# A hybrid decoder trunk on one core: its last stage written as one list of tasks, with the last 512 rows leaving as rows

## The chip, the cores and the metric

One Trainium2 chip, of which the kernel uses one core. The metric is the device time of one execution in microseconds (us). TensorE (PE) multiplies, VectorE (DVE), ScalarE (ACT) and GpSimd (POOL) work on the results, and SyncE (SP) and ACT issue the transfers.

## The reference

Two layers over 1024 tokens of width 1024, all in float32: an RG-LRU block with a SwiGLU network, then stick-breaking attention with a SwiGLU network, and a last RMS norm.

```python
def rms_norm(x, g):
    y = xf * lax.rsqrt(jnp.mean(xf * xf, axis=-1, keepdims=True) + RMS_EPS)
    return y * g
def swiglu_ffn(x, w_in, w_out):
    gu = jnp.einsum("bsd,df->bsf", x, w_in)
    h = jax.nn.silu(gu[..., :D_FF]) * gu[..., D_FF:]
    return jnp.einsum("bsf,fd->bsd", h, w_out)
# per layer:
h = h + mixed                       # RG-LRU (layer 0) or attention (layer 1)
h = h + swiglu_ffn(rms_norm(h, ffn_norm[layer]), ffn_w_in[layer], ffn_w_out[layer])
# at the end:
return rms_norm(h, final_norm)
```

D_FF is 2816. What the change touches is the end of the last SwiGLU network (the product with ffn_w_out) and the last norm.

## The kernel before

The residual h lies in the on-chip memory transposed: tile `h[d][n]` holds 128 columns of the model (block d of 8) by 512 tokens (half n of 2). Every operand of a product is split into a high and a low part of reduced float32, and a product of two such operands is three matmuls (`mm3`: high by high, high by low, low by high), each 128x128 by 128x512 where nothing else is said.

The products of the two SwiGLU networks save one in eight by Strassen's scheme on 2x2 blocks (Winograd's form): seven products, numbered 0 to 6, for eight. A product is summed in a PSUM bank (`BANK`: products 0, 2, 4 and 5 follow one another in one bank, 3 and 6 in another, 1 in a third); behind each product `post_out` adds the bank to h, so the next product in a bank waits until that has been read. Weights are summed and split for them by `Weights` (s12, s2, s3, do_s4 make the sums; a_hi/a_lo, b_hi/b_lo, c_hi/c_lo, d_hi/d_lo the parts; tiles wah, wal, wbh, wbl, wch, wcl, wd). The second matrix is worked off in 13 visits (`VISITS`): visit (d, p0, p1) is the column blocks d and d + 4 with the planes p0 to p1 of the hidden width, a plane being two blocks of 128. A visit of four planes is 84 matmuls, of three 63. The planes' operands come by DMA from a scratch in HBM (`bring`, issued by SP as soon as PE has read the place for the last time) and are split by ACT and DVE (`split_op`: a cast `vh<-vl` and a subtraction) at fixed steps of a visit. The order of PE, ACT, DVE and POOL is that of the code, written out by hand; SP's is set by the scheduler of the language.

The last two visits of layer 1, (3, 8, 11) and (0, 9, 11), are worked off by `finish`: the first with the seven products, the second, with two planes, in plain products `last` (12 matmuls each), so that pieces of it fill PE while the norm is prepared. In it

- `finished(d, n)` squares h[d][n] on ACT, adds the square to `acc[n]` on DVE and multiplies h by the gain of the last norm on ACT;
- `stats` sums acc over the partitions with four one-column matmuls against ones (each counts as two in the trace) and works out the factor 1/rms of each token in a few small steps of DVE and one root of ACT (whose table is loaded at the start of `finish`);
- `factor` spreads the factors over the partitions by matmuls (tile `ob`), `give` multiplies h by them on DVE, or on POOL for some blocks, and stores h transposed (`out_t`).

The first 768 tokens leave the chip transposed. For the last 256, h is transposed on PE (`turn`, 16 transposes), the factor is multiplied in where the banks are read (`y`), and they leave as rows (`out_r`). The host puts the two parts together. `last` is done in three pieces of tokens: all of half 0, the first 256 of half 1, the last 256 of half 1, for the column blocks 0 and 4 each.

Of the kernel before, what the change touches and what calls it, by code (L numbers as in the profile page):

```python
# [16 lines left out]
P = 128  # L17
# [13 lines left out]
LATE = S - 2 * P  # L31
# [318 lines left out]

@with_exitstack
def trunk(
# [11 lines left out]
    ffn_w_out,  # L364
    out,
# [41 lines left out]
    vc = cp.tile([P, P], F32, name="vc")  # L407

# [121 lines left out]
    def gain(h, d, n):  # L530
        nc.scalar.activation(h[d][n], h[d][n], AF.Copy, scale=vc[:, V_FIN + d : V_FIN + d + 1])
# [37 lines left out]
    with ExitStack() as st, tc.manual_schedule(engines={E.PE, E.Activation, E.DVE, E.Pool, E.SP}):  # L569
# [79 lines left out]
        for j in range(3):  # L649
            V.tensor_scalar_mul(nbias[:, :, j], bin_rec, -1.0)  # L650
        column_stats(sacc[1], bank, 1)
# [233 lines left out]
    def mix_out_ffn_in(h, mix, bias, layer, gnext, ob):  # L885
# [131 lines left out]
        with tc.manual_schedule(engines={E.PE, E.Activation, E.DVE, E.Pool}):  # L1017
# [303 lines left out]
            def open_end():  # L1321
                gs.close()
                ep = gs.enter_context(tc.tile_pool(name="ends", bufs=1, reuse_waits="tile"))
                held.append(ep.tile([P, S], F32, name="held"))
                held.extend(ep.tile([P, D], F32R, name=f"we{i}") for i in range(4))
# [50 lines left out]
            def finish(w, e):  # L1376
                u, rs = NV - 2, held[0]
                d1, q0, q1 = VISITS[u]
                d0, p0, p1 = VISITS[u + 1]
                rhs = {i: [R[p][i] for p in range(q0, q1)] for i in range(NPROD)}  # L1380
                banks = {}

                def product(i):
                    new = BANK[i] not in banks
                    if new:
                        banks[BANK[i]] = pp.tile([P, NB], F32, tag="p", name=f"p{i}_ps")
                    part(banks[BANK[i]], w, i, rhs[i], range(len(rhs[i])), onto=not new)
                    return lambda: post_out(u, i, banks[BANK[i]])

                def last(x, n, i0, i1):  # L1390
                    cs = slice(i0 * P, i1 * P)
                    ps = pp.tile([P, NB], F32, tag="p", name="o_ps")[:, cs]
                    for k, p in enumerate(range(p0, p1)):
                        for y in range(2):
                            hi, lo = e.a[("r", y) if x else y]
                            c = slice(k * P, (k + 1) * P)
                            rhs_ = [t[:, cs] for t in R[p][((0, 1), (7, 6))[n][y]]]
                            mm3(ps, hi[:, c], lo[:, c], *rhs_, k + y == 0, k + y == 2)
                    t = h[d0 + x * HK][n][:, cs]
                    V.tensor_add(t, ps, t)  # L1400
                    nc.scalar.square(half(sq, n)[:, cs], t)

                def summed(x, n, i0, i1):
                    cs = slice(i0 * P, i1 * P)
                    t, ac = h[d0 + x * HK][n][:, cs], acc[n][:, cs]
                    V.tensor_add(ac, ac, half(sq, n)[:, cs])
                    nc.scalar.activation(t, t, AF.Copy, scale=vc[:, V_FIN + d0 + x * HK : V_FIN + d0 + x * HK + 1])

                def factor(n, i0, i1):
                    cs = slice(i0 * P, i1 * P)  # L1410
                    spread(half(ob, n), n, i0, i1)
                    nc.scalar.copy(half(rs, n)[:, cs], half(ob, n)[:, cs])

                def give(n, i0, i1, fast, slow=()):
                    cs = slice(i0 * P, i1 * P)
                    for d in (*slow, *fast):
                        t = h[d][n][:, cs]
                        if d in slow:
                            nc.gpsimd.tensor_mul(t, t, half(rs, n)[:, cs])
                        else:  # L1420
                            V.tensor_mul(t, t, half(ob, n)[:, cs])
                        lo = n * NB + i0 * P
                        nc.sync.dma_start(out_t[d][:, lo : lo + (i1 - i0) * P], t)

                first, mid, end = (0, 0, 4), (1, 0, 2), (1, 2, 4)
                root = cp.tile([P, 4], F32, tag="rs_s", name="rs_s", bufs=2)
                nc.scalar.sqrt(root[:, 0:1], ones)
                w.b_lo()
                post = product(0)
                post()  # L1430
                w.c_hi()
                w.c_lo()
                e.a_hi()
                post = product(1)
                post()
                e.a_lo()
                post = product(2)
                post()
                finished(d1, 0)
                w.d_hi()  # L1440
                w.d_lo()
                e.r_hi()
                e.r_lo()
                sq = rp.tile([P, D], F32, tag="raw", name="sq")
                last(0, *first)
                post = product(4)
                summed(0, *first)
                post()
                last(1, *first)
                post = product(5)  # L1450
                summed(1, *first)
                post()
                post = product(3)
                finished(d1 + HK, 0)
                post()
                last(0, *mid)
                stats(acc[0], pp, "p", 0)
                finished(d1 + HK, 1)
                summed(0, *mid)
                post = product(6)  # L1460
                factor(*first)
                give(*first, (), (3, 7))
                post()
                give(*first, (1, 2))
                last(1, *mid)
                finished(d1, 1)
                give(*first, (5,))
                summed(1, *mid)
                last(0, *end)
                give(*first, (0,), (4,))  # L1470
                summed(0, *end)
                stats(acc[1], pp, "p", 1, 0, 2)
                give(*first, (6,))
                last(1, *end)
                factor(*mid)
                give(*mid, (), (3, 7))
                summed(1, *end)
                rows = [(hf, i, pp.tile([P, NB], F32, tag="p", name="e_ps")) for i in range(2, 4) for hf in range(2)]

                def turn(js):  # L1480
                    for hf, i, ps in rows:
                        for j in js:
                            nc.tensor.transpose(
                                ps[:, j * P : (j + 1) * P], h[HK * hf + j][1][:, i * P : (i + 1) * P], ident
                            )

                turn((1, 2, 3))
                give(*mid, (1, 2))
                stats(acc[1], pp, "p", 1, 2, 4)
                turn((0,))  # L1490
                ys = [rp.tile([P, D], F32, tag="raw", name="y") for _ in range(2)]
                for k, (hf, i, ps) in enumerate(rows):
                    y = half(ys[i - 2], hf)
                    r = rcol[:, NT // 2 + i : NT // 2 + i + 1]
                    if k % 2 == 0:
                        nc.scalar.activation(y, ps, AF.Copy, scale=r)
                    else:
                        V.tensor_scalar_mul(y, ps, r)
                    (nc.scalar if k % 2 else nc.sync).dma_start(
                        out_r[(i - 2) * P : (i - 1) * P, hf * NB : (hf + 1) * NB], y  # L1500
                    )
                    if k == 1:
                        give(*mid, (5, 6), (0, 4))

            last_use = {p: max(u for u, (_, p0, p1) in enumerate(VISITS) if p0 <= p < p1) for p in range(NF // 2)}
            for s_, (kind, x) in enumerate(steps[:looped]):
                w, nw, ahead = nw, nxt, None
                if s_ + 2 < len(steps):
                    ahead = weights_of(*steps[s_ + 2])
                    if final and s_ + 3 == len(steps):  # L1510
                        ahead.homes = held[1:]
# [15 lines left out]
                for k, i in enumerate(ORDER):  # L1527
# [79 lines left out]
                    if kind == "v":  # L1607
# [22 lines left out]
            for dn in done:  # L1630
                finished(*dn)
            del done[:]
            if final:
                finish(nw, nxt)
# [364 lines left out]
```

## Time and profile before

| | |
|---|---|
| median of 3 runs | 2187.65 us (2184.54 to 2188.76) |
| the profiled execution, its own time | 2188.74 us |
| its span, first to last instruction | 2187.0 us |
| busy, of the span | PE 99%, weight loads 82%, DVE 78%, ACT 49%, POOL 2% |
| granted TensorE clock, mean | 0.996 |
| product 0 of `finish` starts, in the span | 2139.33 us |

Times of the trace are from the start of its span. In rows of the timeline the first two numbers are the start and the length of an instruction, and the bracket at the end tells how long the engine had been idle and what ended that. A matmul's length includes its way through the array, so successive matmuls overlap; their distance is what PE spends on one. PEld are PE's weight loads.

### The profile page before, as it was taken

The numbers are of one execution on the slowest core, as the hardware profiler recorded it, in microseconds if no ns is written. First come the engines' busy times: TensorE is split into PE (matmuls) and PEld (weight loads), VectorE is DVE, ScalarE is ACT, GpSimd is POOL, SyncE is SP. The second block draws the span as 40 slices with busy tenths as digits, with TensorE's granted clock in tenths as the row PEclk, the third lists the DMA queues.
The fourth block names the chain that finished last, engine by engine and source line by source line (L and its number), as shares of the span: only waits on it lengthen the run. The fifth ranks groups of instructions, "written<-read, shape, count | busy, mean of one in ns | idle before, by whom it ended". The sixth has DMA issues, their size and how long they took to land.

```text
span 2187.0 us, 27244 instructions
## 1 busy us (share of the span) xinstructions
PE 2165.4 (99%) x10054; PEld 1797.8 (82%) x10054; DVE 1707.1 (78%) x2434; ACT 1078.3 (49%) x1776; POOL 35.6 (2%) x44
## 2 busy tenths in 40 slices
PE   9999999999999999999999999999999999999997
PEld 7888888888888888877888888888888888888886
DVE  7978678677777887867888888878867777788786
ACT  5577445334444554644555555544533444454455
POOL 0000020000000000000000000002000000000001
PEclk9999999999999999999999999999999999999999
DMA  4111312344444853444333333541133444476442
GB/s 175 39 49 48 126 39 82 96 140 146 142 146 135 288 188 121 146 117 113 89 104 88 106 87 106 169 165 61 65 109 125 150 142 144 148 242 227 133 136 86
DMA packets 132598, 274.50 MB, mean 126 GB/s; under 512 B 15344, under 2 KB 22640, under 8 KB 132464
## 3 DMA queue, kind: packets, MB, share of 16 engines
q1 hardware_dynamic: 132032, 271.97, 38.4%
q8 instruction: 79, 1.29, 0.2%
q10 hardware_dynamic: 432, 0.79, 0.1%
q14 instruction: 55, 0.45, 0.1%
HBM read 176.75 MB, written 70.78 MB: 113 GB/s over the span
## 4 chain that ended last, share of the span: by engine, by line
PE 94%; DVE 3%; ACT 2%; DMA 0%; issue 0%; SPq 0%; DVEq 0%; ACTq 0%
PE p_ps L446 18%; PE p_ps L444 18%; PE p_ps L445 18%; PE qk_ps L444 4%; PE qk_ps L446 4%; PE qk_ps L445 4%; PE z_ps L1786 3%; PE av_ps L1834 3%; PE wt_ps L1817 3%; PE a_ps L445 3%; PE a_ps L446 3%; PE a_ps L444 3%; PE ob_ps L445 2%; PE ob_ps L444 2%; PE ob_ps L446 2%; PE g_ps L446 1%
## 5 line engine op out<-in xcount | busy, mean ns | idle before, releaser
L444 PE MATMUL p_ps<-vh,wbh 128*128 128x512 f32 x524 | 204.8, 391 | 2.0 <-ACT ta L1362 2.0
L446 PE MATMUL p_ps<-vh,wbl 128*128 128x512 f32 x524 | 204.9, 391 | 0.0
L446 PE MATMUL p_ps<-vh,wcl 128*128 128x512 f32 x524 | 204.1, 390 | 0.5 <-DVE wcl L977 0.5
L445 PE MATMUL p_ps<-vl,wbh 128*128 128x512 f32 x524 | 204.6, 391 | 0.0
L446 PE MATMUL p_ps<-vh,wal 128*128 128x512 f32 x524 | 204.1, 390 | 0.1
L444 PE MATMUL p_ps<-vh,wch 128*128 128x512 f32 x524 | 204.1, 389 | 0.0
L445 PE MATMUL p_ps<-vl,wch 128*128 128x512 f32 x524 | 203.9, 389 | 0.0
L445 PE MATMUL p_ps<-vl,wah 128*128 128x512 f32 x524 | 203.9, 389 | 0.0
L444 PE MATMUL p_ps<-vh,wah 128*128 128x512 f32 x524 | 203.8, 389 | 0.0
L1798 ACT ACTIVATE F<-z_ps 128x512 f32<-128x512 f32 (+3 forms) x188 | 91.6, 488 | 181.2 <-PE z_ps L1786 181.1
L963 ACT CAST wbh<-sb 128x1024 fp32r<-128x1024 f32 (+2 forms) x69 | 69.7, 1010 | 192.5 <-DVE sb L947 192.5
L1805 DVE TENSOR_TENSOR_SCAN F<-F,unit 128x128 f32<-128x128 f32 (+3 forms) x128 | 104.8, 819 | 56.8 <-ACT F L1798 56.3
L444 PE MATMUL qk_ps<-vh,whi 128*128 128x512 f32 x264 | 120.5, 456 | 0.6 <-ACT vh L524 0.6
L444 PEld LDWEIGHTS p_ps<-vh,wbh 128*128 128x128 f32 x524 | 98.6, 188 | 22.8 <-ACT ta L1362 2.5
L446 PEld LDWEIGHTS p_ps<-vh,wbl 128*128 128x128 f32 x524 | 98.8, 188 | 21.7 <-DVE wbl L967 1.2
L446 PEld LDWEIGHTS p_ps<-vh,wcl 128*128 128x128 f32 x524 | 98.3, 188 | 21.6 <-DVE wcl L977 1.3
L446 PEld LDWEIGHTS p_ps<-vh,wal 128*128 128x128 f32 x524 | 98.3, 188 | 21.2 <-DVE wal L958 1.0
L445 PEld LDWEIGHTS p_ps<-vl,wbh 128*128 128x128 f32 x524 | 98.7, 188 | 20.6
L445 PEld LDWEIGHTS p_ps<-vl,wah 128*128 128x128 f32 x524 | 98.4, 188 | 20.5
L445 PEld LDWEIGHTS p_ps<-vl,wch 128*128 128x128 f32 x524 | 98.4, 188 | 20.5
L444 PEld LDWEIGHTS p_ps<-vh,wah 128*128 128x128 f32 x524 | 98.4, 188 | 20.4
L444 PEld LDWEIGHTS p_ps<-vh,wch 128*128 128x128 f32 x524 | 98.4, 188 | 20.4
(375 smaller groups left out, 5481.0 us busy)
## 6 DMA issues: line engine op xcount, KB each, us to landing
raw<-in_ffn_w_in SPq DMA_DIRECT2D x88, 512.0 KB, 3.7
vl<-pd SPq DMA_DIRECT2D x128, 256.0 KB, 3.3
pd<-U SPq DMA_DIRECT2D x90, 256.0 KB, 2.3
raw<-in_ffn_w_out SPq DMA_DIRECT2D x28, 512.0 KB, 4.0
raw<-in_attn_w_qkv SPq DMA_DIRECT2D x24, 512.0 KB, 4.0
kh<-qh SPq DMA_DIRECT2D x64, 128.0 KB, 2.3
kl<-ql SPq DMA_DIRECT2D x64, 128.0 KB, 2.3
acc<-pd SPq DMA_DIRECT2D x28, 256.0 KB, 2.6
```

The costliest lines, as they stand in the source:

```text
L444: nc.tensor.matmul(ps, lhsT=wh, rhs=mh, start=first, stop=False, **kw)
L445: nc.tensor.matmul(ps, lhsT=wh, rhs=ml, start=False, stop=False, **kw)
L446: nc.tensor.matmul(ps, lhsT=wl, rhs=mh, start=False, stop=last, **kw)
L963: nc.scalar.copy(self.full(self.wb), self.full(self.sb))
L1786: nc.tensor.matmul(ps[:, 0:n], lhsT=lhsT, rhs=rhs, start=i == 0, stop=i == 1)
L1798: nc.scalar.activation(F, Z.pop(c)[:, 0:n], AF.Sigmoid, scale=-SC)
L1805: V.tensor_tensor_scan(rev, rev, unit[:, NB - n :][:, ::-1], 0.0, op0=ALU.mult, op1=ALU.add)
L1817: nc.tensor.transpose(tp[:, c : c + P], F[:, (kb % 4) * P : (kb % 4 + 1) * P], ident)
L1834: nc.tensor.matmul(ps[:, c:], lhsT=VV[q][:, kb, hx], rhs=t.pop(u)[:, c:], start=kb == 4 * G and i == 0, stop=kb == 3 and i == 1,)
```

## The change

The last two visits are written as a list of tasks with engine, assumed cost, dependences and rank (`end_plan`), from which the class `Plan` (used for the first stages before) makes the order of each engine. What is done differs as well:

- All of half 1, 512 tokens, now leaves as rows (`LATE` is 512). The second visit's product for half 1 (`lower`) takes the hidden planes as the stationary and the weights as the moving operand, 256 columns in two runs of 128, so that its result has tokens on the partitions, and sums it in the bank onto transposes of h made there just before (`turned`: 32 transposes instead of 16). Each of the four row blocks of 128 tokens then gets the sum of squares of those 256 columns from ACT (`row_sum`, a square with a sum output), root, factor, and its output in four pieces on DVE and ACT (`row_out`); the blocks are stored as 512 KB each, the last in two halves. The gains of columns 0 and 4 come in there, as a row `gr` loaded from a new input `fin`; for half 1 they carry a factor -0.5 that saves a step in the factor.
- Half 0 is done as before, but its eight multiplications are all on DVE, and stored one block (256 KB) at a time. POOL has no work in the stage.
- DVE adds each bank to h directly (`onto_h`); ACT no longer copies banks for it in this stage.
- The weights of the second visit have tiles of their own; their loads and the load of the table for the root are written in visit (2, 8, 11), the last before `finish`. In the order that comes out, the table load stands there, and the loads, and the cast of the high parts, stand in visit (3, 0, 4), seven visits earlier.
- A tile `tiny` of 256 bytes a partition is added among the constants.

```diff
-LATE = S - 2 * P
+LATE = NB
+def end_plan(plan, fn, d0, d1, left):
...
+    halved = plan.add("dve", 0.4, fn["half", 0], [], 8)
+    bl = plan.add("dve", 0.92, fn["b_lo", 0], [], 0)
+    for d, n in left:
+        normed(d, n, None, 3)
+    ch = plan.add("act", 0.95, fn["c_hi", 0], [bl], 6)
+    cl = plan.add("dve", 1.1, fn["c_lo", 0], [ch], 6)
+    el = []
+    for x in range(2):
+        eh = plan.add("act", 0.5, fn["e_hi", x], [], 1)
+        el.append(plan.add("dve", 0.62, fn["e_lo", x], [eh], 1))
+
+    p = prod(0, [], 0)
+    h = post(0, p, 2)
...
+    def finish_row(i, dep, tdep, r):
+        s = plan.add("act", 0.5, fn["rsum", i], [dep], r - 8)
+        m = plan.add("dve", 0.2, fn["rmean", i], [s, m1], r - 8)
+        t = plan.add("act", 0.22, fn["rroot", i], [s, m1], r - 8)
+        f = plan.add("dve", 0.6, fn["rfac", i], [t, m], r - 8)
...
+    for i in range(2, 4):
+        deps = [f6, m1] if i == 2 else muls
+        t = mm(0.86, ("T", i, (1, 2, 3, 0)), deps, 24 + 2 * i)
+        finish_row(i, mm(1.46, ("low", i), [], 24 + 2 * i), t, 24 + 2 * i)
...
+    tiny = cp.tile([P, 64], F32, name="tiny")
...
-                root = cp.tile([P, 4], F32, tag="rs_s", name="rs_s", bufs=2)
-                nc.scalar.sqrt(root[:, 0:1], ones)
...
+                def lower(i):
+                    ps = rows[i, 0][:, 0 : 2 * P].rearrange("p (x c) -> p x c", x=2)
+                    for k, y_ in order:
+                        ah, al = (t[:, i * P : (i + 1) * P] for t in R[p0 + k][(7, 6)[y_]])
+                        wh, wl = (flat(t)[:, :, 2 * y_ + k] for t in (hi, lo))
+                        kw = dict(start=False, skip_group_check=True)
+                        nc.tensor.matmul(ps, lhsT=ah, rhs=wh, stop=False, **kw)
+                        nc.tensor.matmul(ps, lhsT=ah, rhs=wl, stop=False, **kw)
+                        nc.tensor.matmul(ps, lhsT=al, rhs=wh, stop=(k, y_) == order[-1], **kw)
...
+                def row_sum(i):
+                    nc.scalar.activation(junk, rows[i, 0][:, 0 : 2 * P], AF.Square, accum_out=one(s4, i))
...
+                def row_store(i, js):
+                    c = slice(js[0] * P, js[-1] * P + P)
+                    dst = pairs(out_r[i * P : (i + 1) * P])[:, :, c]
+                    (nc.sync if js[0] == 0 else nc.scalar).dma_start(dst, pairs(y[i])[:, :, c])
...
+                end_plan(Plan(pe=0.0, act=0.3, dve=1.0, dma=0.0), Steps(acts), d0, d1, done).emit()
...
+                            d, p0, p1 = VISITS[NV - 1]
+                            for y in range(2):
+                                src = ffn_w_out[layer, d + y * HK][:, :, p0 * P : p1 * P]
+                                nc.sync.dma_start(held[5 + y].rearrange("p (y c) -> p y c", y=2), src)
+                            nc.sync.dma_start(held[3][:, 0 : 2 * P], fin.broadcast_to([P, 2 * P]))
+                            nc.scalar.sqrt(tiny[:, 62:63], ones)
```

PE's order in the stage is now: products 0, 1, 2, upper 0 (half 0 of column block 0), 4, upper 1 (of block 4), 5, 3, eight transposes, sums of half 0, two thirds of product 6, the spread, the rest of 6, two transposes, lower 0, two transposes, lower 1, sums of half 1, four transposes, then eight transposes and lower 2, and eight transposes and lower 3.

DVE at the start of the stage, before; `hh_0` is half 0 and `hh_1` half 1 of h, `acc` the sums of squares, `ta` the copy of product 0's bank, `we` are the parts of the second visit's weights.

```order
L1366 TENSOR_TENSOR hh_0_13011<-p_ps,hh_0_13011 128x512
L521 TENSOR_TENSOR acc_13016<-acc_13016,rbc_82 128x512
L521 TENSOR_TENSOR acc_13015<-acc_13015,rbc_81 128x512
L967 TENSOR_TENSOR wbl<-sb,wbh 128x2x384
L1366 TENSOR_TENSOR hh_0_13005<-ta,hh_0_13005 128x512
L977 TENSOR_TENSOR wcl<-s_18207,wch 128x384
```

DVE at the same place with the change:

```order
L1474 TENSOR_TENSOR hh_0_13014<-p_ps,hh_0_13014 128x512
L626 TENSOR_TENSOR acc_13019<-acc_13019,rbc_84 128x512
L1074 TENSOR_TENSOR wbl<-sb,wbh 128x2x384
L1607 TENSOR_TENSOR we_17124<-end_17127,we_17123 128x512
L1607 TENSOR_TENSOR we_17124<-end_17128,we_17123 128x512
L1504 TENSOR_TENSOR hh_0_13008<-hh_0_13008,p_ps 128x512
L1601 TENSOR_TENSOR acc_13018<-acc_13018,rbc_83 128x512
```

One addition to acc has moved behind the addition of product 0 to h, and both low parts of the second visit's weights have moved ahead of it; that addition reads the bank itself.

PE around the sums of half 1, before; `o_ps` is a bank of `last`, and of the two operands the one before the comma is the moving, the other the stationary one.

```order
L445 MATMUL o_ps<-vl_0_13076,we_17123 128x256
L446 MATMUL o_ps<-vh_0_13075,we_17122 128x256
L510 MATMUL st_ps<-ones,acc_13016 128x1 x2
L444 MATMUL o_ps<-vh_3_13543,we_17121 128x256
L445 MATMUL o_ps<-vl_3_13544,we_17121 128x256
```

PE around the sums of half 1 with the change; `e_ps` is a bank of a row block, and moving and stationary operand have changed places.

```order
L1533 MATMUL e_ps<-we_17124,vh_0_13078 128x256
L1534 MATMUL e_ps<-we_17123,vl_0_13079 128x256
L1540 MATMUL st_ps<-ones,acc_13019 128x1 x4
L1521 MATMUL e_ps<-ident,hh_1_13009 128x128
L1521 MATMUL e_ps<-ident,hh_1_13017 128x128
```

All four sums stand in one place, behind lower 0 and lower 1 and ahead of the last transposes of these two row blocks, where before two of them stood between two pieces of `last`, and the other two behind the transposes.

ACT in visit (3, 0, 4), before; the two copies into `held` are those of its products 3 and 4, the casts are of planes for the next visit.

```order
L1297 CAST vh_3_13535<-vl_3_13536 128x512
L1362 COPY held<-p_ps 128x512
L1297 CAST vh_0_13045<-vl_0_13046 128x512
L1297 CAST vh_1_13047<-vl_1_13048 128x512
L1362 COPY held<-p_ps 128x512
```

ACT at the same place with the change:

```order
L1404 CAST vh_3_13538<-vl_3_13539 128x512
L1470 COPY held<-p_ps 128x512
L1404 CAST vh_0_13048<-vl_0_13049 128x512
L1404 CAST vh_1_13050<-vl_1_13051 128x512
L1604 CAST we_17123<-end_17127 128x512
L1604 CAST we_17123<-end_17128 128x512
L1470 COPY held<-p_ps 128x512
```

The casts of the second visit's weights have come in ahead of the copy of product 4. Their loads stand in SP's queue among the loads of the planes, the second one behind the load of the plane whose place is freed within product 3.

More of the change, by code (lines that the diff above doesn't have):

```diff
@@ L1384, in product @@
                     new = BANK[i] not in banks
                     if new:
[L1386 to L1412, printed above, removed]
@@ L1439, in finish @@
[L1439 to L1469, printed above, removed]
@@ L1470, in finish @@
[L1470 to L1484, printed above, removed]
-                            )
@@ L1487, in finish @@
[L1487 to L1496, printed above, removed]
-                    else:
[L1498 to L1503, printed above, removed]
+                        banks[BANK[i]] = bank(f"p{i}_ps")
@@ new lines, in turned @@
+                def turned(i, js):
+                    for j in js:
+                        new = (i, j // 2) not in rows
+                        if new:
+                            rows[i, j // 2] = bank("e_ps") if i < 3 else half(ob, j // 2)
+                        for x in range(2):
+                            c = (2 * (j % 2) + x) * P
+                            nc.tensor.matmul(
+                                rows[i, j // 2][:, c : c + P], lhsT=h[j + HK * x][1][:, i * P : (i + 1) * P], rhs=ident,
+                                is_transpose=True, start=new and x == 0, stop=True, skip_group_check=True,
+                            )
@@ new lines, in sums, with mean @@
+                def sums(n):
+                    if n == 0:
+                        banks["st"] = bank("st_ps")
+                    for i in range(4):
+                        nc.tensor.matmul(
+                            banks["st"][:, 4 * n + i : 4 * n + i + 1],
+                            lhsT=acc[n][:, i * P : (i + 1) * P], rhs=ones, start=True, stop=True,
+                        )
+                def mean(n):
+                    V.tensor_scalar(
+                        m4[:, 4 * n : 4 * n + 4], banks["st"][:, 4 * n : 4 * n + 4], 1.0 / D, EPS, op0=ALU.mult, op1=ALU.add
+                    )
@@ L1629, in mix_out_ffn_in @@
                         open_last()
[L1630 to L1634, printed above, removed]
+            if not final:
+                for dn in done:
+                    finished(*dn)
+                del done[:]
+        if final:
+            with tc.manual_schedule(engines={E.PE, E.Activation, E.DVE, E.Pool, E.SP}):
+                finish(nw)
         gs.close()
```

204 lines of the change are left out of this document (173 added, 31 removed).

## The prediction

> **What bounds the kernel now.** I read the page first, then a table of busy time by stretch over the last stage, then the timelines of the engines at each gap of PE.
>
> ```profile
> span 2187.0 us, 27244 instructions
> PE 2165.4 (99%) x10054; PEld 1797.8 (82%) x10054; DVE 1707.1 (78%) x2434; ACT 1078.3 (49%) x1776; POOL 35.6 (2%) x44
> 2139.30:2143.50 4.20, 4.20 (x19) 3.19 (x17) 3.89 (x8) 3.17 (x5) 0.00 (x0) 1.00 0.13 29
> 2143.50:2145.60 2.10, 0.07 (x1) 0.00 (x0) 0.93 (x3) 2.08 (x5) 0.00 (x0) 1.00 0.19 67
> 2145.60:2149.30 3.70, 3.69 (x9) 2.91 (x10) 2.81 (x5) 1.29 (x3) 0.00 (x0) 0.54 0.01 4
> 2149.30:2169.30 20.00, 19.96 (x113) 17.32 (x112) 12.58 (x25) 11.28 (x21) 2.20 (x2) 1.00 0.00 2
> 2169.30:2172.40 3.10, 0.00 (x0) 0.00 (x0) 2.72 (x4) 1.46 (x3) 1.57 (x2) 1.00 0.84 313
> 2172.40:2176.50 4.10, 4.09 (x20) 3.81 (x21) 3.12 (x11) 1.55 (x4) 0.00 (x0) 0.59 0.61 222
> 2176.50:2178.90 2.40, 2.38 (x22) 2.14 (x20) 1.39 (x5) 0.98 (x3) 1.68 (x3) 0.99 0.27 99
> 2178.90:2183.40 4.50, 0.00 (x0) 0.00 (x0) 3.45 (x9) 1.37 (x2) 1.10 (x2) 1.00 0.81 282
> ```
>
> PE is busy for 99% of the span, so the change can only win where PE stands. After length, the columns are busy time of PE, PEld, DVE, ACT and POOL, then PE's granted clock, DMA share and GB/s. In the last 47.7 us, which the change rewrites, PE has two gaps, of 2.1 and 3.1 us, each with a stretch at about half clock behind it (0.54, 0.59), and a tail of 8.1 us (2178.9 to 2187.0) without it. What ended the gaps:
>
> ```profile
> 2145.61 0.63 PE L444 MATMUL p_ps<-vh,wbh 128*128 128x512 f32 x1 [2.03 <-ACT ta L1362]
> 2172.41 0.60 PE L510 MATMUL st_ps<-ones,acc 128*128 128x1 f32 x4 [3.14 <-DVE acc L1406]
> 2143.58 1.28 ACT L1427 ACT_TABLE_LOAD   x1
> 2144.99 0.57 ACT L1362 COPY ta<-p_ps 128x512 f32<-128x512 f32 x1
> 2169.68 1.74 DVE L521 TENSOR_TENSOR acc<-acc,rbc 128x512 f32<-128x512 f32 x1 [1.00 <-ACT rbc L520]
> 2167.10 3.77 POOL L1419 TENSOR_TENSOR hh<-hh,held 128x512 f32<-128x512 f32 x3 [638.20 <-ACT held L1412]
> ```
>
> The first gap: product 2 sums onto the bank of product 0, whose copy by ACT stands behind a table load. The second: the column sums of half 1 wait for DVE, where one addition took 1.74 us while POOL multiplied.
>
> **The first gap, after.** The table load moves into the visit before, and the bank is read by DVE alone. DVE's rows now decide:
>
> ```profile
> 2141.86 0.68 DVE L521 TENSOR_TENSOR acc<-acc,rbc 128x512 f32<-128x512 f32 x1
> 2143.46 0.95 DVE L967 TENSOR_TENSOR wbl<-sb,wbh 128x768 fp32r<-128x768 f32 x1
> 2145.58 0.69 DVE L1366 TENSOR_TENSOR hh<-ta,hh 128x512 f32<-128x512 f32 x1 [1.17 <-ACT ta L1362]
> 2146.19 0.55 DVE L977 TENSOR_TENSOR wcl<-s,wch 128x384 fp32r<-128x384 f32 x1
> 2139.33 0.39 PE L444 MATMUL p_ps<-vh,wah 128*128 128x512 f32 x1
> 2143.19 0.39 PE L446 MATMUL p_ps<-vh,wal 128*128 128x512 f32 x1
> ```
>
> A 128x512 addition is followed by the next after 0.61 us (2145.58 to 2146.19); wbl takes 0.87 by its width (0.95 less the 0.08 by which an addition's 0.69 overlaps its follower). DVE is free of the same addition at 2141.86 + 0.61 = 2142.47. Then come wbl (to 2143.34), two low parts of the last weights (2144.55) and the addition that frees the bank (0.69: 2145.24). PE starts product 2 at 2145.27 instead of 2145.61: only **0.34 us** gained. The two low parts, placed ahead by a plan that takes DVE as free 1.0 us after product 0's start when it is so 3.1 us after it (2139.33), replace the table load. The gap is then 1.7 us (from 2143.58). Does the clock fall behind it? It fell after 2.03 us; that row is the nearest, so I take that it falls, which costs what it costs now. If not, 3.41 us at half clock go, 1.7 us more gained. [...]
>
> **From product 2 to PE's last instruction.** Row durations:
>
> ```profile
> 2168.03 0.28 PE L444 MATMUL o_ps<-vh,we 128*128 128x256 f32 x1
> 2168.15 0.28 PE L445 MATMUL o_ps<-vl,we 128*128 128x256 f32 x1
> 2162.37 0.95 PE L510 MATMUL st_ps<-ones,acc 128*128 128x1 f32 x8
> 2165.34 1.05 PE L491 MATMUL ob<-ident,rcol 128*128 128x128 f32 x8
> 2176.57 1.47 PE L1483 MATMUL e_ps<-ident,hh 128*128 128x128 f32 x12
> ```
>
> A 512-column matmul comes every 0.227 us (18 of products 0 and 1 from 2139.33 to 2143.19), a 256-column one every 0.12, a transpose every 0.11 (1.47 less the last one's drain of some 0.16, by 12); four column sums take 0.85, four spreads 0.9. After: 60 matmuls of 512 columns (13.6: products 4, 5, 3 and 6 of 9, two upper blocks of 12), 48 of 256 (5.76), 32 transposes (3.5), two sums (1.7), one spread (0.9), in all 25.5 us. Before: the same 108 matmuls, 16 transposes, 6 spreads. What may still stop PE: the sums of half 0 wait for addition, square and addition behind product 5 (0.69 + 0.64 + 0.69, some 2.2 with hand-overs), under product 3 (2.04) and eight transposes (0.87), so 0.7 is spare. The factors of half 0 (some 1.5 behind the sums) lie under six matmuls (1.36): 0.2 of wait. The sums of half 1, today's 3.14 us, wait for the addition onto h of product 6, its square, two multiplications and the last addition, some 3.2 us behind product 6; under T, low 0, T, low 1 lie 3.3. Without that cover it costs up to the 3.1 of today. The eight multiplications of half 0 are all DVE's now, and POOL no longer slows it. So from product 2's end 25.7 us, where before it was 2149.27 to 2178.88, 29.6: **3.9 us** gained, mostly the 3.1 gap and the 1.7 behind it, less 16 transposes (1.8), with two spreads (0.45) and the short stalls between small matmuls on top.
>
> Last matmul: 2149.27 - 0.34 + 25.7, rounded 2174.8.
>
> **The tail.** Before, sums, factor and four outputs ended in these rows:
>
> ```profile
> L486 DVE TENSOR_TENSOR rcol<-rs_s,rs_t 128x2 f32<-128x2 f32 (+1 forms) x3 | 0.5, 160 | 0.1
> L1400 DVE TENSOR_TENSOR hh<-o_ps,hh 128x256 f32<-128x256 f32 x4 | 1.7, 419 | 0.2
> L1401 ACT ACTIVATE sq<-hh 128x256 f32<-128x256 f32 x4 | 1.7, 417 | 7.1 <-DVE hh L1400 7.1
> 2183.01 0.41 SPq L1499 DMA_DIRECT2D out<-y  x1
> 2184.00:2185.00 1.00, 0.00 (x0) 0.00 (x0) 0.00 (x0) 0.00 (x0) 0.00 (x0) 0.50 1.05 380
> ```
>
> After: square with its sum 0.5 (0.42 plus hand-over; the sum output is not in the trace: 0.4 to 0.65), root 0.2, four small DVE steps 0.8 (0.16 each, next 0.2 on), two outputs of 256 columns each on DVE and ACT (0.42 + 0.34): the last store is issued 2.3 us behind the last matmul, at 2177.1. From the last issue to the end it took 4.0 (2183.01 to 2187.0). Rows 2 and 3, 1.05 MB, are then still in the queues, 2.8 us at 380 GB/s from some 1.3 us behind their first issue at 2176.2, so I add 0.5. Row 3's outputs also wait until row 0's store (issued 2172.8) has left its buffer, one of three; a 512 KB store has no row; loads of 256 and 512 KB land in 3.3 and 3.7 (rows below), so it leaves at some 2176.1 to 2176.8 and the outputs, due at 2176.2, wait 0 to 0.6; I take 0, and keep 0.6 for the range. End 2181.6: the tail falls from 8.1 to 6.8, **1.3 us**.
>
> **Ahead of the last stage.** The loads of the last weights now stand in SP's queue during visit 3, and ACT's two casts of them between the copies of its products 3 and 4 (the last pair of order rows in the change's section):
>
> ```profile
> 2005.84 0.32 SPq L1293 DMA_DIRECT2D vl<-pd  x1
> 2007.97 1.14 ACT L1297 CAST vh<-vl 128x512 fp32r<-128x512 f32 x2
> 2010.15 0.59 ACT L1362 COPY held<-p_ps 128x512 f32<-128x512 f32 x1 [1.04 <-PE p_ps L446]
> 2004.00:2006.00 2.00, 2.00 (x10) 1.65 (x10) 0.67 (x2) 1.29 (x3) 0.00 (x0) 1.00 0.95 335
> vl<-pd SPq DMA_DIRECT2D x128, 256.0 KB, 3.3
> raw<-in_ffn_w_in SPq DMA_DIRECT2D x88, 512.0 KB, 3.7
> ```
>
> The second load is issued behind the row of 2005.84, at some 2006.3; with 3.3 us to land, or 0.7 more in a DMA that is 0.95 busy, it is there at 2009.6 to 2010.8 (two loads of 256 KB are 1.4 us at 380 GB/s), the cast ends 0.6 later, and the copy that stands behind it ends at 2011.2 to 2012. What is queued behind the casts is that copy and all of ACT's later work; PE waits for the copy. The product that needs its bank starts near 2012.8 (2010.1 + 2.72), so 0.8 us or more is spare: cost **0**, bounds 0 and 3 (a load 2 us later, and a half-clock stretch of 1.7). Also at nothing: the table load, on an ACT that is busy for 49% of the span (1.3 if it should hold a bank's copy), and DVE's one 128x8 multiplication at the start.
>
> **The sum.** 0.3 + 3.9 + 1.3, and 0.1 lost to rounding: 5.4 us. The profiled execution took 2188.74 (span 2187.0 and 1.74 around it), after: 2183.3. The median of before is 1.1 lower, so 2187.65 - 5.4, rounded **2182.2 us**. What a measurement of this kernel can tell from no change is about 0.2%, 4.4 us: faster means below 2183.3.
>
> **Rivals.** (1) *The clock falls again in the tail of PE*: T, sums and low alternate there. [...] By the rows, 3.4 us of work at half clock cost 1.7: 2183.9. Against it: 2176.50 to 2178.90 held only transposes and sums, then PE stood still, and the clock was still 1.00 until 2183.4. [...] Chance 0.10. (2) *ACT waits in visit 3* for the early load: PE stalls, upper bound 3: 2185.2. For it: a DMA 0.95 busy; against it the 0.8 spare. 0.12. (3) *The moving operand in two runs of 128* (low): no row shows one. If it streamed at half rate, 48 x 0.12 = 5.8, 2188.0, no change; nothing in the rows excludes it or a part. 0.08. (4) *Slower*: a new 256-byte tile in front of nearly all other tiles shifts their addresses, for the whole program. If that cost a matmul 1.0 ns of 227, 10054 x 1.0 = 10 us, 2192.3, and from there on it decides. Against it: matmuls on quite different tiles agree within 2 ns:
>
> ```profile
> L444 PE MATMUL p_ps<-vh,wbh 128*128 128x512 f32 x524 | 204.8, 391 | 2.0 <-ACT ta L1362 2.0
> L444 PE MATMUL p_ps<-vh,wah 128*128 128x512 f32 x524 | 203.8, 389 | 0.0
> ```
>
> 0.07. That the change does nothing is excluded by the order of instructions. The forecast keeps 0.63, mostly 2180.5 (no fall of the clock) to 2183.3. Range: 2180.0 to 2187.0, to take in rivals 1 and 2 and most of 3. Faster 0.62 (the forecast, less a little of its upper end, and part of 1), same 0.31, slower 0.07.
>
> **What would show it.** Right: a gap of about 1.7 us before product 2, ended by DVE; no gap over 0.5 from there to the last matmul; 6.8 us from the last matmul to the end. Wrong: a gap in visit 3 ended by ACT; 256-column matmuls on e_ps further apart than 0.12; matmul means above 391; a clock of 0.5 in the last 10 us of PE.

## The result, and the profile after

The changed kernel takes **2183.4 us** (median of 22 runs, 2180.92 to 2187.61), the kernel before beside it 2187.4 (22 runs): 4.0 us less, a ratio of 0.9983 (95% interval 0.9976 to 0.9990). Timed again later, beside other runs of the kernel before, it was 2.9 us less (0.9984, 0.9975 to 0.9993), where 3 to 5 were expected. The forecast was 2182.2, in a range of 2180.0 to 2187.0. By the first comparison the change is 0.17% faster, a little less than the 0.2% that "faster" (0.62) asked for, so by the prediction's own measure the outcome is "same", to which it gave 0.31; the interval excludes no change all the same.

The profiled execution took 2181.98 us. The head of its page, then busy time by stretch over the last stage, with the columns of the table shown of before (length, PE, PEld, DVE, ACT, POOL, PE's clock, DMA share, GB/s):

```profile
span 2180.0 us, 27248 instructions
PE 2162.8 (99%) x10066; PEld 1795.6 (82%) x10066; DVE 1704.7 (78%) x2435; ACT 1077.2 (49%) x1781; POOL 29.1 (1%) x38
```

```profile
2138.30:2142.55 4.25, 4.25 (x19) 3.19 (x17) 4.25 (x8) 3.22 (x6) 0.00 (x0) 1.00 0.00 0
2142.55:2144.35 1.80, 0.00 (x1) 0.03 (x1) 1.80 (x4) 0.84 (x3) 0.00 (x0) 1.00 0.00 0
2144.35:2146.45 2.10, 2.10 (x9) 1.75 (x10) 2.10 (x5) 0.98 (x2) 0.00 (x0) 1.00 0.03 8
2146.45:2166.40 19.95, 19.95 (x113) 17.03 (x112) 11.93 (x24) 8.36 (x16) 0.00 (x0) 1.00 0.07 26
2166.40:2166.85 0.45, 0.04 (x2) 0.04 (x1) 0.45 (x2) 0.45 (x3) 0.00 (x0) 1.00 0.95 350
2166.85:2172.95 6.10, 6.10 (x52) 5.92 (x52) 5.57 (x20) 3.56 (x13) 0.00 (x0) 1.00 0.70 264
2172.95:2180.00 7.05, 0.02 (x1) 0.00 (x0) 2.22 (x8) 2.50 (x8) 0.00 (x0) 0.80 0.73 273
```

The two gaps, from the timeline of PE:

```profile
2144.35 0.47 PE L549 MATMUL p_ps<-vh,wbh 128*128 128x512 f32 x1 [1.80 <-DVE hh L1504]
2166.82 1.05 PE L1540 MATMUL st_ps<-ones,acc 128*128 128x1 f32 x8 [0.41 <-DVE acc L1601]
```

The stage, from product 0's first matmul to the end of the span, fell from 47.67 us (2139.33 to 2187.0) to 41.69 (2138.31 to 2180.0): 0.24 up to product 2's start, 1.6 in product 2 (full clock behind the gap), 3.1 from there to the last matmul, 1.1 in the tail. The 3.14 us gap is 0.41. But the program ahead of the stage lost 1.0 us, which is told below.

Spans can't simply be subtracted from one another. Besides the stage, PE's clock also falls to 0.50 for 3.41 us at a time near 958 and 992 us (once near 39) in some executions and not in others, of both kernels (twice in the first profile of before, once in this one, and in one of the experiments for twice 3.41 us at both places). So the profiles are compared from a fixed point behind that: ACT's copy of product 3 in visit (3, 0, 4), which starts at 2007.49 in the kernel before and 2005.45 in this one.

| kernel | that copy to product 0 of the stage | stage | both | median less before's, same runs | ratio, 95% interval |
|---|---|---|---|---|---|
| before | 131.84 | 47.67 | 179.51 | | |
| before, second profile | 131.87 | 47.56 | 179.43 | | |
| changed | 132.86 | 41.69 | 174.55 | -4.0 | 0.9976 to 0.9990 |
| changed, again | 132.87 | 41.67 | 174.54 | -2.9 | 0.9975 to 0.9993 |
| table load early (before) | 131.89 | 45.20 | 177.09 | -1.5 | 0.9984 to 1.0002 |
| low parts later | 132.99 | 40.43 | 173.42 | -5.6 | 0.9969 to 0.9987 |
| row 3 apart | 133.06 | 41.65 | 174.71 | -3.9 | 0.9977 to 0.9994 |
| low parts later, row 3 apart | 133.03 | 40.51 | 173.54 | -6.0 | 0.9964 to 0.9982 |
| load late | 131.88 | 41.68 | 173.56 | -5.2 | 0.9970 to 0.9987 |
| load late, low parts later | 131.85 | 40.43 | 172.28 | -6.5 | 0.9963 to 0.9982 |
| the same, two on POOL | 131.86 | 40.51 | 172.37 | -5.8 | 0.9961 to 0.9981 |
| three on POOL | 132.78 | 42.43 | 175.21 | one run | |
| without row 1's store | 132.87 | 41.48 | 174.35 | one run | |
| longer gap | 133.54 | 44.55 | 178.09 | -0.6 | 0.9986 to 1.0004 |

Kernels that share a stretch agree in its column within 0.3 us, far closer than the medians do. One stands apart: in the longer gap's profile the early load came later than elsewhere, and the way to the stage is 133.54.

### The profile page after: what moved, and what is told of

It reads as the page before. It is cut to its first block, busy times and chain, and to the rows that moved or that the text cites. A ratio compares the mean times of both kernels' runs of the same rounds, so it can differ in the third digit from the quotient of the medians.

```text
span 2180.0 us, 27248 instructions
## 1 busy us (share of the span) xinstructions
PE 2162.8 (99%) x10066; PEld 1795.6 (82%) x10066; DVE 1704.7 (78%) x2435; ACT 1077.2 (49%) x1781; POOL 29.1 (1%) x38
## 4 chain that ended last, share of the span: by engine, by line
PE 93%; DVE 4%; ACT 2%; issue 1%; DMA 1%; SPq 0%; DVEq 0%; ACTq 0%
PE p_ps L551 18%; PE p_ps L549 18%; PE p_ps L550 18%; PE qk_ps L549 4%; PE qk_ps L551 4%; PE qk_ps L550 4%; PE z_ps L1935 3%; PE av_ps L1983 3%; PE wt_ps L1966 3%; PE a_ps L550 3%; PE a_ps L551 3%; PE a_ps L549 3%; PE ob_ps L550 2%; PE ob_ps L549 2%; PE ob_ps L551 2%
```

## The experiments

### The gap before product 2

**Low parts later** (e1): DVE frees product 0's bank ahead of the last weights' low parts.

```diff
-        el.append(plan.add("dve", 0.62, fn["e_lo", x], [eh], 1))
+        el.append(plan.add("dve", 0.62, fn["e_lo", x], [eh], 3))
-                end_plan(Plan(pe=0.0, act=0.3, dve=1.0, dma=0.0), ...
+                end_plan(Plan(pe=0.0, act=0.3, dve=3.1, dma=0.0), ...
```

> The changed kernel, with the plan told that DVE is free 3.1 us after product 0's start (1.0 before) and with a later rank for the two low parts of the last weights, so that DVE adds product 0 to h ahead of them. Theory A (the gap before product 2 is DVE's queue): the gap falls from 1.8 to 0.6 us, product 2 starts 1.2 us earlier, and with no fall of the clock there in the changed kernel's usual run the median falls by 1.2 us, to 2182.2. Theory B (in most runs the clock does fall behind the 1.8 us gap): 1.7 us more, 2180.5, and the slow end of the runs (2187) goes. Rival (upper block 0 now waits for the low parts): a new gap of up to 1.2 us ahead of it, no change.

Measured: 2180.82 us, 5.6 below before. Its profiled span is 2183.2, longer than the changed kernel's: it has 13.7 us at half clock ahead of the stage (6.83 us each near 957 and 991; its granted clock is 0.996, that of the changed kernel's profile 0.999). PE's timeline has

```profile
2147.61 0.47 PE L549 MATMUL p_ps<-vh,wbh 128*128 128x512 f32 x1 [0.60 <-DVE hh L1504]
```

and no new wait ahead of upper block 0. The stage is 1.26 us shorter, so theory A holds: the gap was DVE's queue, as the prediction had it.

**Table load early** (b1): this part of the change alone, in the kernel before.

```diff
-                nc.scalar.sqrt(root[:, 0:1], ones)      # at the start of finish
+                        if final and x == NV - 3 and k == 0:
+                            nc.scalar.sqrt(root[:, 0:1], ones)
```

> The kernel before, with one part of the change alone: the table load of the root stands in the visit ahead of the last stage. Theory A (the load held the copy of product 0's bank): the copy and product 2 come 1.3 us earlier, the gap is 0.75 instead of 2.03 us, and without a fall of the clock behind it product 2 takes 2.1 instead of 3.7 us: the median falls by 3.0 us, to 2184.4, three quarters of what the whole change gave. If the clock behind that gap does not fall in most runs of the kernel before: 1.3 us, to 2186.1. Rival (the load in the visit before holds a copy there): up to 1.3 us are given back.

Measured: 1.5 us below before, its interval reaching to none. In the profile the gap is 0.55 us, at full clock, and the stage 2.5 us shorter; product 2 is followed by a new wait of 0.29 for a part of the last weights. The mechanism is as expected; the median gained half of the 3.0 expected. The profile isn't typical of this kernel's runs: it has a granted clock of 0.998, eight of the eleven runs have 0.996, that is more time at half clock, and where they spent it is not on record.

**A longer gap** (e6): product 0's addition gets rank 5 instead of 2, with DVE free at 3.1.

```diff
-    h = post(0, p, 2)
+    h = post(0, p, 5)
...
-                end_plan(Plan(pe=0.0, act=0.3, dve=1.0, dma=0.0), ...
+                end_plan(Plan(pe=0.0, act=0.3, dve=3.1, dma=0.0), ...
```

> The changed kernel, with product 0's addition to h put one DVE addition later, so that the gap before product 2 is 2.4 us instead of 1.8 (the two low parts and one addition to acc stand ahead of it). Theory A (whether the clock falls hangs on how the idle time lies in the free-running windows of 3.41 us, so a longer gap makes the fall likelier but not sure): the stage is 0.6 us longer, and 1.7 more where the clock falls; median 0.6 to 2.3 us above the changed kernel's, that is 1.7 to 3.4 below the kernel before. Theory B (a threshold of gap length between 1.8 and 2.03 us): the clock always falls, 2.3 us above. [...]

Measured: 2185.7 us, 0.6 below before where the changed kernel is 2.9 to 4.0 below. The gap became 3.12 us and not 2.4 (the addition of product 1 to h slipped ahead too), and the clock fell behind it:

```profile
2147.01 0.72 PE L549 MATMUL p_ps<-vh,wbh 128*128 128x512 f32 x1 [3.12 <-DVE hh L1504]
```

A gap of this length doesn't tell theory A from B. The profiles side by side tell more. In each the half-clock stretches ahead of PE's last matmul last 3.41 us (in one profile twice that) and start on one grid of 3.413: in the first profile of before at 957.99, 992.12, 2145.82 and 2173.13, that is 10, 338 and 8 such steps apart. Two windows of that grid in three kernels, the one that holds the gap and the one behind it: before, the kernel without row 1's store (the change's gap of 1.80, by chance whole in one window), and the longer gap:

```profile
2142.42:2145.83 3.41, 1.38 (x7) 0.84 (x6) 1.93 (x4) 3.36 (x6) 0.00 (x0) 1.00 0.28 77
2145.83:2149.24 3.41, 3.41 (x9) 2.62 (x9) 2.58 (x5) 1.06 (x3) 0.00 (x0) 0.50 0.02 5
```

```profile
2143.11:2146.52 3.41, 1.61 (x8) 1.05 (x7) 3.41 (x7) 1.35 (x4) 0.00 (x0) 1.00 0.02 5
2146.52:2149.93 3.41, 3.41 (x16) 2.83 (x16) 2.71 (x6) 1.70 (x3) 0.00 (x0) 1.00 0.00 0
```

```profile
2143.65:2147.06 3.41, 0.28 (x3) 0.08 (x1) 3.38 (x7) 1.23 (x4) 0.00 (x0) 1.00 0.00 0
2147.06:2150.47 3.41, 3.41 (x8) 2.68 (x9) 2.11 (x5) 1.59 (x3) 0.00 (x0) 0.50 0.02 5
```

PE busy for 1.38 us of a window: half clock in the next. Busy for 1.61: full clock. At this place the line lies between 1.8 and 2.03 us of standing still within one window. None of the six profiles with the 1.80 us gap shows a fall behind it, but in five of them a line of the grid cuts the gap, so the one above is the only test of 1.80 us in one window. Nor is PE's busy time what decides everywhere: in the profile without row 1's store the window from 955.28 to 958.69 has PE busy for 2.47 us, and the next is at half clock; the one from 986.00 to 989.41 has 2.20, and the next is at full clock. What is counted there stays open.

**Before again** (e10), to see whether the grid decides.

> The kernel before itself, for one more profile of its two gaps in the last stage (2.03 and 3.14 us), both of which had cost clock in the first profile. Theory A (the clock falls for one window of 3.41 us when PE stood still for more than some 1.8 us of the window ahead, on a free-running grid): whether it falls hangs on where the grid lies; with the boundary inside the 2.03 us gap there is no fall and product 2 takes 2.1 us instead of 3.7, with the boundary in the middle third of the 3.14 us gap none there. So the stage is 47.7 us with both falls, 46.0 with one, 44.3 with none. Rival (the length of the gap decides): both fall again, 47.7.

Measured: a stage of 47.56 us, both falls there again:

```profile
2144.31 0.79 PE L444 MATMUL p_ps<-vh,wbh 128*128 128x512 f32 x1 [2.03 <-ACT ta L1362]
2171.10 0.61 PE L510 MATMUL st_ps<-ones,acc 128*128 128x1 f32 x4 [3.14 <-DVE acc L1406]
```

The grid's lines lay at 2140.91 and 2144.32, so the 2.03 us were whole in one window once more, and this run doesn't tell the theories apart. That a gap of 2.03 cut by a line costs no clock was not seen.

### Ahead of the stage

**Load late** (e4): the last visit's weights go to a tile of the ring of raw weights, which comes free only in visit (2, 8, 11).

```diff
+                            er = rp.tile([P, D], F32, tag="raw", name="er")
                             for y in range(2):
-                                nc.sync.dma_start(held[5 + y]..., src)
+                                nc.sync.dma_start(half(er, y)..., ...); held[5 + y] = half(er, y)
```

> The changed kernel, with the weights of the last visit loaded into a tile of the ring of raw weights, so that their load and the two casts on ACT stand in visit (2, 8, 11), the last ahead of the stage, and no longer in visit (3, 0, 4). Theory A (in visit (3, 0, 4) ACT waits 1.31 us for the second load, the copy behind it keeps DVE idle for 1.61 us, and DVE, which is busy without a break for the 20 us that follow, hands that on to PE some 15 us later): the waits of PE for wd and wal near 2023 to 2029 us shrink to what the kernel before has there, the stage's start comes 1.0 us earlier, and the whole stands 5.0 us below the kernel before instead of 4.0. Rival (the pauses there belong to something else, such as DMA for the planes): they stay, and nothing is gained; or the late load holds a cast on ACT in front of a copy in visit (2, 8, 11), and up to 1 us is given back there.

Measured: 5.2 us below before, and from the fixed point to the stage 131.88 instead of 132.86: all of the 1.0 us is back, and nothing is lost in visit (2, 8, 11). The chain in the changed kernel, by the timelines of ACT, DVE and PE's weight loads:

```profile
2008.91 0.62 ACT L1604 CAST we<-end 128x512 fp32r<-128x512 f32 x1 [1.31 <-DMA end<-in_ffn_w_out]
2009.44 0.58 ACT L1470 COPY held<-p_ps 128x512 f32<-128x512 f32 x1
2010.05 0.69 DVE L1474 TENSOR_TENSOR hh<-held,hh 128x512 f32<-128x512 f32 x1 [1.61 <-ACT held L1470]
2024.36 0.19 PEld L551 LDWEIGHTS p_ps<-vh,wd 128*128 128x128 f32 x1 [0.46 <-DVE wd L1093]
2029.11 0.19 PEld L551 LDWEIGHTS p_ps<-vh,wal 128*128 128x128 f32 x1 [0.79 <-DVE wal L1065]
```

and the stretch in which DVE had no time to catch up, of the changed kernel and with the load late:

```profile
2020.00:2030.00 10.00, 9.61 (x41) 7.09 (x40) 10.00 (x17) 5.08 (x10) 0.00 (x0) 1.00 0.61 189
```

```profile
2020.00:2030.00 10.00, 10.00 (x45) 8.03 (x44) 10.00 (x17) 5.92 (x11) 0.00 (x0) 1.00 0.60 188
```

PE never waited for that copy. DVE did, and DVE is busy for 10.0 of 10.0 us there, so most of the 1.3 us of ACT's delay reached PE fifteen to twenty microseconds later as late weight parts (41 matmuls instead of 45 in this stretch, 1.0 us by the start of the stage).

### From the sums to the end

**Three multiplications on POOL** (e5), as before.

```diff
-                    "mul": lambda d, x: V.tensor_mul(...),
+                    "mul": lambda d, x: (nc.gpsimd if x == 1 else V).tensor_mul(...),
```

> The changed kernel, with three of half 0's eight multiplications on POOL, as the kernel before had. Theory A (POOL's work slows DVE's additions, which made the 3.14 us wait of the sums of half 1): DVE's additions beside POOL take over 1.2 us instead of 0.68, PE's wait for the sums of half 1 grows from 0.4 to 1.0 or more. Rival (the wait was DVE's queue alone): DVE has three instructions less in front of the sums, and the wait goes to 0.

Measured in one run: the stage is 42.43 us, 0.74 longer. PE, DVE and POOL:

```profile
2167.23 1.05 PE L1540 MATMUL st_ps<-ones,acc 128*128 128x1 f32 x8 [1.11 <-DVE acc L1601]
2164.59 0.68 DVE L1642 TENSOR_TENSOR hh<-hh,ob 128x512 f32<-128x512 f32 x1
2165.37 1.80 DVE L1601 TENSOR_TENSOR acc<-acc,rbc 128x512 f32<-128x512 f32 x1
2162.83 3.79 POOL L1642 TENSOR_TENSOR hh<-hh,held 128x512 f32<-128x512 f32 x3 [636.11 <-ACT held L1641]
```

Theory A. Beside POOL, DVE's multiplication with one operand in PSUM (ob) takes 0.68 us, its addition of two operands in SBUF 1.80. In the changed kernel, with no work on POOL, the same addition takes 0.68 (from 2166.08); why POOL's work lengthens the one and not the other was not shown. The wait went from 0.41 to 1.11 us only, where before it was 3.14: POOL accounts for 0.7 of the 2.7 us by which the change shortened it. The other 2.0 came with the new order of PE and DVE and with the whole of half 1 being worked off in rows, and no run takes these apart.

**Row 3 apart** (e2): the last row block's outputs ran strictly in turn, each waiting for the one before, on DVE, ACT, DVE, ACT:

```profile
2174.54 0.48 DVE L1586 SCALAR_TENSOR_TENSOR y<-ob,rcol,end 128x256 f32<-128x256 f32 x1
2175.06 0.47 ACT L1590 ACTIVATE y<-ob,rcol 128x256 f32<-128x256 f32 x1 [0.53 <-DVE y L1586]
2175.57 0.48 DVE L1588 TENSOR_SCALAR y<-ob,rcol 128x256 f32<-128x256 f32 x1 [0.54 <-ACT y L1590]
2176.09 0.47 ACT L1590 ACTIVATE y<-ob,rcol 128x256 f32<-128x256 f32 x1 [0.55 <-DVE y L1588]
2176.59 0.64 ACTq L1595 DMA_DIRECT2D out<-y  x1
```

```diff
...
-                            rows[i, j // 2] = bank("e_ps") if i < 3 else half(ob, j // 2)
+                            rows[i, j // 2] = half(ob, 0) if i == 3 and j < 2 else bank("e_ps")
...
-                        y[i] = rp.tile([P, D], F32, tag="raw", name="y")
+                        y[i] = held[0] if i == 3 else rp.tile([P, D], F32, tag="raw", name="y")
```

> The changed kernel, with row block 3's four outputs taken apart: its second bank is one of the ring instead of the other half of the tile ob, its output lies in a tile that no store holds, DVE makes pieces 0 and 1, ACT pieces 2 and 3. Theory A (the four outputs run in turn because both engines read the one tile ob, and this lengthens the tail): the last issue comes 1.1 us earlier behind the last matmul (2.6 instead of 3.7), and the median falls by 1.0 us, to 2182.4. Rival (the tail is set by the bytes in the queues): the outputs run side by side, the end moves by less than 0.3 us.

Measured: 3.9 us below before, the stage 41.65: nothing gained, theory A's gain is refuted. The outputs do run side by side (bank, output tile and engines were changed at once, so which of them had held them in turn is not shown), and the last issue stands 4.3 us ahead of the end (2175.99 of 2180.3) instead of 3.4 (2176.59 of 2180.0). Where the earlier issue went shows in the issues of the last 8 us: one of the two halves takes 3.3 us to land, not 2.5.

```profile
out<-y SPq DMA_DIRECT2D x1, 256.0 KB, 2.5
out<-y ACTq DMA_DIRECT2D x1, 256.0 KB, 2.5
```

```profile
out<-held ACTq DMA_DIRECT2D x1, 256.0 KB, 2.7
out<-held SPq DMA_DIRECT2D x1, 256.0 KB, 3.3
```

**Both** (e3), row 3 apart and low parts later:

> Both edits, low parts later and row 3 apart. If they are independent, the median falls by 1.2 + 1.0 = 2.2 us below the changed kernel's 2183.4, to 2181.2; if the clock often fell behind the 1.8 us gap, by up to 3.9, to 2179.5. If one hides the other, by no more than 1.2.

Measured: 6.0 us below before; by the stage (40.51 against 40.43) it is the low parts alone.

**Without row 1's store** (e8), on the kernel with row 3 apart:

```diff
-                    (nc.sync if js[0] == 0 else nc.scalar).dma_start(...)
+                    if i != 1: (nc.sync if js[0] == 0 else nc.scalar).dma_start(...)
```

> The kernel with row block 3 apart, with the store of row block 1 (512 KB) left out, so 128 rows of the output are not written; all else as there. It tells why taking row 3 apart issued its stores 0.9 us earlier and ended no earlier. Theory A (the stores of the last 8 us fill the queues, at some 390 GB/s): 512 KB less end the stage 1.0 to 1.3 us earlier, at some 40.5 us after product 0's start instead of 41.65, with the last issue at the same place. Rival (a fixed time from the last issue to the end, 4.3 us): the stage stays at 41.6.

Measured in one run: a stage of 41.48 us, 0.17 shorter, the landing of the last halves 2.7 and 3.3 as before. So row 1's bytes don't hold the end: the queues stand still for a while ahead of row 2's bytes either way (0 GB/s for 0.15 us from 2175.65 with row 1's store, for 1.4 us from 2175.0 without it). What the last stores can then still wait for are one another and row 2's, 1 MB within some 3 us; a run without row 2's store was not made, so that is argued, not shown.

### The version that beats both

**Load late and low parts later** (e7), the edits of e4 and e1:

> Late load and late low parts together (e4 and e1). If the two costs are independent, 4.0 + 1.0 + 1.2 = 6.2 us below the kernel before, or 6.6 if the gain of the late low parts (5.6 below) repeats. If the late load brings ACT a wait in front of the stage, no better than the late low parts alone.

Measured: **2179.72 us**, 6.5 below before (ratio 0.9973, 0.9963 to 0.9982); both stretches are the shorter ones (131.85 and 40.43), 2.3 us less than the changed kernel in the profile, so the two costs are independent.

**The same with two multiplications on POOL** (e9):

```diff
+                    "mul": lambda d, x: (nc.gpsimd if d in (d1, 6) else V).tensor_mul(...),
```

> Late load and late low parts, with two of half 0's eight multiplications on POOL. With three, POOL was busy until 2166.6 us and DVE's last addition to acc, begun at 2165.4, took 1.80 us beside it. Two should end 1.3 us earlier, ahead of that addition. Theory A (POOL costs only where an addition of two operands in SBUF meets it): the addition takes 0.68 and starts some 0.6 us earlier, PE's wait of 0.4 for the sums of half 1 goes, DVE has 1.2 us less to do ahead of the row blocks, the stage becomes 0.4 to 1.0 us shorter than with late load and low parts alone (40.4 or so), median 0.4 to 1.0 lower. Rival (POOL's work meets the addition all the same): it takes 1.2 or more, no gain or 0.5 us lost.

Measured: 2179.95 us (0.9971, 0.9961 to 0.9981), no clear difference from the version above. POOL is done at 2163.24, DVE's addition starts there and takes 0.69 us, PE's wait for the sums of half 1 is gone, and the last issue comes 0.4 us earlier behind product 2's start (31.84 against 32.24 us), but the stage is 40.51, 0.08 longer. Once more an earlier last issue did not end the kernel earlier; what ends the span there stays open.

## Why the prediction was right or wrong

- **The first gap.** Right in cause and size: 1.80 us by DVE (1.7 foretold), product 2 0.24 us earlier (0.34). The step that failed is "that row is the nearest, so I take that it falls": the clock did not fall, so the case without a fall was the true one, and 1.6 us more were gained in the profile.
- **Product 2 to PE's last instruction.** 26.5 us instead of 25.7. The sums of half 1 wait 0.41 (none foretold: "3.2 under 3.3" had no room for hand-overs), and the first 256-column matmul behind transposes comes after some 0.2 instead of 0.12, four times. Rivals 1, 3 and 4 are refuted by the trace: full clock to PE's end, 256-column matmuls 0.12 apart, matmul means of 390 ns, not above 391:

```profile
2171.86 0.28 PE L1533 MATMUL ob<-we,vh 128*128 128x256 f32 x1
2171.98 0.28 PE L1534 MATMUL ob<-we,vl 128*128 128x256 f32 x1
...
L549 PE MATMUL p_ps<-vh,wbh 128*128 128x512 f32 x524 | 204.3, 390 | 1.8 <-DVE hh L1504 1.8
```

- **The tail.** 7.0 us, 6.8 foretold, by two errors that cancel: the last issue came 3.6 us behind the last matmul and not 2.3, since the outputs ran in turn (2.0 us instead of 0.8), and the end 3.4 us behind that issue and not 4.5. The experiment on row 3 shows that the two hang together: what the issue gains, the landing loses.
- **Ahead of the last stage.** This step failed: "cost 0", because the copy had 0.8 us to spare before PE needed its bank. That was so, and PE had no wait there. But the copy is DVE's to read as well, and DVE has next to no spare time in the next 20 us (busy for 9.95 of 10 us from 2010 and for 10.00 from 2020): 1.0 us. It was rival 2, with its cause and place of origin right, and its path missed.
- **The sum.** In the profiles the change gains 5.0 us (179.51 to 174.55) where 5.4 were foretold: 0.24 + 1.6 + 3.1 + 1.1 in the stage, less 1.0 ahead of it. That the two are so close is luck: 1.6 too little for the first gap stand against 0.1, 0.8 and 0.2 too much in the other terms of the stage and the 1.0 ahead of it. (The prediction's last matmul has a slip as well: 2149.27 - 0.34 + 25.7 is 2174.6, not 2174.8.) The medians gained 4.0 and 2.9, and the interval of each holds 5.0. The granted clocks on record show a reason why medians may gain less than profiles: among the runs of the kernel before, timed beside the changed kernel the second time, one has 0.999 and the shortest span, 2182.0 us, two have 0.995, and spans of 2186.8 on average. With rounding, 0.999 leaves that run at most 6.6 us at half clock, less than two windows of 3.41, so at least one of the stage's two falls, which both profiles of before show, was missing in it. How often that happens was not shown.

## What to carry to other kernels

When an early load or cast is put in front of other work of an engine (here ACT's copy of a bank behind a cast that waited 1.31 us for its load), ask not only whether the engine that bounds the kernel waits there, but whether any engine between them is busy without a break behind it: such an engine can pass most of a delay on long afterwards (here 1.0 of 1.3 us). A planner's due times decide what stands ahead of what: two numbers in the plan (DVE free at 3.1 instead of 1.0, a rank of 3 instead of 1) were worth 1.3 us in the stage. And in a tail that ends in stores, issuing the last one earlier need not end the kernel earlier: 0.9 us in one experiment and 0.4 in another gained nothing, for a reason that the runs don't show.

## What the runs showed of the hardware

- The stretches at half clock ahead of PE's last matmul last 3.41 us (twice that at two places of one profile) and start on a grid of 3.413 us, whose lines lie elsewhere in each profile (near product 2 at 2145.83 and 2144.32 in the two profiles of the kernel before, at 2147.06 in that of the longer gap). Ahead of product 2, PE still for 1.80 us of a window left the next at full clock (one profile), 2.03 us halved it (two profiles), and the fall there cost some 1.6 us of PE's work (product 2 took 3.7 us instead of 2.1). Near 958 and 992 us PE's busy time doesn't order the windows in this way (busy for 2.47 us: half clock next; for 2.20: full).
- A stretch of 6.1 us with many transposes and 256-column matmuls kept the clock at 1.00 (2166.85 to 2172.95).
- A square with a sum output on ACT is two instructions; the second, in the groups of ACT over the last stage, takes 0.20 us:

```profile
L1563 ACT ACTIVATION_READ_ACCUMULATOR end<-e_ps 128x1 f32 x3 | 0.6, 202 | 0.0
```
